# Key loads of the next attention head: all at once, or one with each tile of queries

## The chip, the cores and the metric

The kernel runs on one core of a Trainium2 chip. The metric is the device time of one launch in microseconds (us), the median over several runs. The engines are TensorE (PE, matmuls), VectorE (DVE), ScalarE (ACT), GpSimd (POOL) and SyncE (SP, which here only issues transfers).

## What is computed

One inference step of a one-layer encoder. 16 + 2048 prompt positions and 8 × 16 sample positions of width 1024 are normed and projected by one matrix; eight attention heads of 64 with forget gates, and a short gated convolution beside them, are joined by an output projection. The part that matters here is the attention of the prompt, whose logit has the running sum `c` of the log forget values in it:

```python
p = jnp.einsum('bld,dn->bln', h, w_in)
q, k, v, za, fl, bg, cg, hc, zc = jnp.split(p, SPLIT_IDX, axis=-1)
logf = jax.nn.log_sigmoid((fl + b_f).astype(jnp.float32))
...
s = jnp.einsum('bqhd,bkhd->bhqk', qblk, k) * (DH ** -0.5)
s = s + cq[...] - ck[...]                       # c = cumsum(logf)
s = jnp.where(kpos <= qpos, s, -jnp.inf)
p = jax.nn.softmax(s, axis=-1)
o = jnp.einsum('bhqk,bkhd->bqhd', p, v)
...
cat = jnp.concatenate([o_a * silu(za), y_c * silu(zc)], axis=-1)
xp = xp + jnp.einsum('blm,md->bld', cat, w_out)
```

## The kernel before

All is in float32, each product made of parts in a rounded type (high and low part: `hh`/`hl` of the normed rows, `wh`/`wl` of the weights, `kh`/`kl` of the keys, `qh`/`ql` of the queries). The work runs in two groups of positions. Group 0 is the positions 0 to 1279, group 1 the other 784 with the 128 sample rows. In each group the projection makes queries, keys and values and stores them to DRAM (`qh_d`, `ql_d`, `kh_d`, `kl_d`, `v_d`, the running sums `c_d`) through POOL's queue; attention reads them back.

Attention goes by units of 256 queries: a unit is a head h and a block u, with two tiles of 128 queries. Group 0 has u = 0 to 4 for each of eight heads, 40 units, and unit number n is head (n − 1) // 5, u = (n − 1) % 5; group 1 has u = 5 to 7, units 41 to 64. For each unit a query load of three 64-partition pieces fills `qa` (`qh` twice) and `qb` (`ql`), and two short ones put the sums into `qb`; both tiles are double-buffered by unit. For each head a key load fills `ka` (`kh` and `kl`) and `kb` (`kh`), with two short ones for the sums; these are double-buffered by head. A piece is 64 × 1280 elements in group 0 (320 KB) and 64 × 2064 in group 1 (516 KB). `vb` holds the values of one head. The scores `sp` are two matmuls, `kb` with `qb` and `ka` with `qa`.

Between the attention's steps, PE does the projection of later columns (`ps` from `hh`, `hl`, `wh`, `wl`). Its weights come in blocks `raw` of 512 KB whose loads ACT issues; ACT casts one to `wh`, DVE makes `wl`. All other loads are on SP's queue (q1 in the profile; ACT's is q10, POOL's stores are q0). In turn the loads of SP and ACT take eight semaphores, and each load waits for the one eight before it to have landed.

What sets the order: the kernel is a set of generators, and class `Times` (line 68) keeps a model of each engine's time. `weave` (line 215) lets that generator go on whose next step is ready first by the model, which fixes PE's order; `settle` (line 235) sorts the instructions of each other engine, and SP's transfers, by their time in the model. So a transfer that is asked for at another place changes the model's times and with them the order on every engine. All instructions are recorded through one helper, which is why every row of the profile has line L278.

`scores_of` (line 965) is the generator that asks for keys and queries. When it comes to unit n it asks for the keys of the head itself and of the next one, `load_head` (line 905), and for the queries of this unit and the next, `load_queries` (line 953).

Of the kernel before, what the change touches and what calls it, by code (L numbers as in the profile page):

```python
# [18 lines left out]
DRAM = bass.MemoryType.DRAM  # L19

P = 128
# [5 lines left out]
DH = 64  # L27
# [287 lines left out]
class Step:  # L315
# [4 lines left out]
        for k, v in args.items():  # L320
            setattr(self, k, v)

    def dma(self, out, in_):

        if out.dtype == F32R:
            out = out.bitcast(F32)
        if in_.dtype == F32R:
            in_ = in_.bitcast(F32)
        return getattr(self.nc, STORES if out.space == DRAM else "sync").dma_start(out=out, in_=in_)

    def open(self, ctx, name, side=None, space=None):
        k = {}
# [47 lines left out]
    def load_constants(self, pool):  # L380
        nc, dma = self.nc, self.dma
        mraw = pool.tile([P, P], F32, name="mraw")
        dma(out=mraw, in_=self.cst[:, C_MASK:C_MASK + P])
        nc.vector.tensor_copy(out=self.mask, in_=mraw)
        for i in range(3):
            dma(out=self.cw[:, :, i], in_=self.conv_w[0, i].rearrange("(c p) -> p c", p=P))

        nc.vector.tensor_scalar(out=self.cw, in0=self.cw, scalar1=0.5, scalar2=None, op0=ALU.mult)
# [22 lines left out]
    def normalise(self, ph, xp, bufs, beside=()):  # L411
# [7 lines left out]
        def prepare():  # L419
            i, (pos, rows, ct, col) = todo.pop(0)  # L420
            xt = xp.tile([P, D], F32, name="xt", bufs=bufs)
            if pos == 0:
                dma(out=xt[:NMETA], in_=self.meta_tokens)
                dma(out=xt[NMETA:], in_=self.x_p[:P - NMETA])
            else:
                dma(out=xt[:rows], in_=self.x_s if pos == NPOS else self.x_p[pos - NMETA:pos - NMETA + rows])
            if pos == p0:
                dma(out=g_bc, in_=self.norm_g[0].partition_broadcast(P))
            if beside:
                beside.pop(0)()  # L430
            sq = xp.tile([P, D], BF16, name="sq")
            ss = xp.tile([P, 1], F32, name="ss", bufs=4)
            nc.scalar.activation(out=sq[:rows], in_=xt[:rows], func=AF.Square, accum_out=ss[:rows])
            self.rsqrt(ss[:rows])
            nc.vector.scalar_tensor_tensor(out=xt[:rows], in0=xt[:rows], scalar=ss[:rows, 0:1], in1=g_bc[:rows],
                                           op0=ALU.mult, op1=ALU.mult)
            ahead.append((xt, rows, ct, col, i))
# [465 lines left out]
                self.dma(out=out[a:a + 1, full * P:n], in_=c[t0 + full:t0 + full + 1, :n % P])  # L903

    def load_head(self, ph, h):
        dma = self.dma
        npos = GROUPS[0][1] if ph == 0 else NPOS
        i, p, rows = h % 2, h // 2, slice(DH * (h % 2), DH * (h % 2) + DH)
        ka, kb = self.ka[i], self.kb[i]
        dma(out=ka[0:DH, :npos], in_=self.kh_d[p][rows, :npos])  # L910
        dma(out=ka[DH:P, :npos], in_=self.kl_d[p][rows, :npos])
        dma(out=kb[BR:, :npos], in_=self.kh_d[p][rows, :npos])
        self.sums_rows(kb[2:4], h, 0, self.nk)

    def load_values(self, ph, h):

# [48 lines left out]
    def scores_of(self, ph, st, ready):  # L965

        nc = self.nc
        units = st["units"]
        loaded, asked = 0, 0
        while ph not in self.summed:  # L970
            yield lambda: 0.0 if ph in self.summed else NEVER
        for n, (h, u) in enumerate(units):
            while ("q", h // 2) not in ready:
                yield lambda: 0.0 if ("q", h // 2) in ready else NEVER

            for ahead in range(2):
                if loaded < H and loaded <= h + ahead and ("k", loaded // 2) in ready:
                    self.load_head(ph, loaded)
                    loaded += 1
                if asked < len(units) and asked <= n + ahead and ("q", units[asked][0] // 2) in ready:  # L980
                    self.load_queries(ph, asked, st)
                    asked += 1
            qa, qb, ka, kb = self.qa[n % 2], self.qb[n % 2], self.ka[h % 2], self.kb[h % 2]
            done = []
            for c0, m, nk in self.query_tiles(u):
                while st["tiles"] - st["turned"] >= SB[ph]:
                    yield lambda: 0.0 if st["tiles"] - st["turned"] < SB[ph] else NEVER
                st["tiles"] += 1
                sl = self.ap.tile([P, min(self.nk, NPOS)], F32, name="s", bufs=SB[ph])
                mx = self.ap.tile([P, 8], F32, name="nm", bufs=16)  # L990
                blocks = (nk + P - 1) // P
                nch = (nk + 511) // 512
                ends = [min(nk, (blocks * (x + 1) // nch) * P) for x in range(nch)]
                k0 = 0
                for x, k1 in enumerate(ends):
                    w = k1 - k0
                    yield self.when(qa, qb, ka, kb, slot=(self.sps, "sp"))
                    sp = self.sps.tile([P, 512], F32, name="sp", bufs=SPB)
                    diag = k1 == nk
                    nc.tensor.matmul(sp[:m, :w], qb[:, c0:c0 + m], kb[:, k0:k1], start=True, stop=False)  # L1000
                    nc.tensor.matmul(sp[:m, :w], qa[:, c0:c0 + m], ka[:, k0:k1], start=False, stop=not diag)
                    if diag:
                        nc.tensor.matmul(sp[:m, w - m:w], self.identr[:, :m], self.mask[:, :m], start=False, stop=True)
                    nc.vector.tensor_scalar(out=sl[:m, k0:k1], in0=sp[:m, :w], scalar1=1.0, scalar2=None, op0=ALU.mult,
                                            op1=ALU.max, accum_out=mx[:m, x:x + 1])
                    k0 = k1
                nm = mx[:, 6:8]
                nc.vector.tensor_reduce(out=nm[:m, 0:1], in_=mx[:m, :nch], axis=AX.X, op=ALU.max, negate=True)
                nc.scalar.activation(out=sl[:m, :nk], in_=sl[:m, :nk], func=AF.Exp, bias=nm[:m, 0:1], accum_out=nm[:m, 1:2])
                nc.vector.reciprocal(out=nm[:m, 1:2], in_=nm[:m, 1:2])  # L1010
                done.append((sl, nm))
            st["scored"].append(done)
# [548 lines left out]
STORES = "gpsimd"  # L1561
# [38 lines left out]
BR = 4  # L1600
# [38 lines left out]
```

## Time and profile before

| | us |
|---|---|
| median of 3 runs | 1683.21 (1681.59 to 1683.66) |
| profiled execution, its own time | 1680.57 |
| its span | 1678.7, at a mean granted clock of 0.972 |
| busy: PE / DVE / ACT / POOL | 1564.9 / 861.0 / 632.5 / 481.2 |
| loads on SP's queue, ACT's, stores on POOL's | 106.38, 30.94, 66.96 MB |

The profile is one execution. PE is the engine that is busy nearly all the time; a stretch in which it waits, with what ended the wait, is read from its timeline. The granted clock is TensorE's, as a share of full speed.

### The profile page before, as it was taken

The numbers are of one execution on the slowest core, as the hardware profiler recorded it, in microseconds if no ns is written. First come the engines' busy times: TensorE is split into PE (matmuls) and PEld (weight loads), VectorE is DVE, ScalarE is ACT, GpSimd is POOL, SyncE is SP. The second block draws the span as 40 slices with busy tenths as digits, with TensorE's granted clock in tenths as the row PEclk, the third lists the DMA queues.
The fourth block names the chain that finished last, engine by engine and source line by source line (L and its number), as shares of the span: only waits on it lengthen the run. The fifth ranks groups of instructions, "written<-read, shape, count | busy, mean of one in ns | idle before, by whom it ended". The sixth has DMA issues, their size and how long they took to land.

```text
span 1678.7 us, 27726 instructions
## 1 busy us (share of the span) xinstructions
PE 1564.9 (93%) x10311; PEld 1452.5 (87%) x10311; DVE 861.0 (51%) x2276; ACT 632.5 (38%) x1196; POOL 481.2 (29%) x750
## 2 busy tenths in 40 slices
PE   4789999998999989899995999999999999999996
PEld 4779999998999978899984998998898999868885
DVE  4525667336667557552332666776576673212221
ACT  4314555325553322411111655555554553111221
POOL 2543435523211421225041313212121121223322
PEclk9899999999999998999997999999999999999998
DMA  7446653475432676522237534535534231364442
GB/s 193 118 120 158 155 142 111 113 191 139 105 77 55 219 222 194 153 53 76 40 83 155 137 101 125 127 92 158 140 67 114 37 85 31 88 232 135 142 138 88
DMA packets 159143, 206.06 MB, mean 123 GB/s; under 512 B 22220, under 2 KB 123108, under 8 KB 156320
## 3 DMA queue, kind: packets, MB, share of 16 engines
q1 hardware_dynamic: 73952, 106.38, 22.2%
q10 hardware_dynamic: 61360, 30.94, 11.9%
q0 software_dynamic: 23696, 66.96, 11.5%
q8 instruction: 82, 1.34, 0.3%
q14 instruction: 53, 0.43, 0.1%
HBM read 137.28 MB, written 66.93 MB: 122 GB/s over the span
## 4 chain that ended last, share of the span: by engine, by line
PE 73%; DMA 11%; issue 6%; POOL 3%; DVE 3%; ACT 2%; SPq 1%; ACTq 0%; POOLq 0%; DVEq 0%
PE ps L278 45%; PE sp L278 10%; PE o L278 9%; PE tp L278 8%; DMA raw<-in_w_in_dram 3%; PE tr L278 1%; DMA sqk_d<-el 1%; DMA vb<-v_d 1%; SPq L278 1%; DMA qb<-ql_d 1%; DMA cat_d<-kf 1%; DMA vn<-in_cache_v_dram 1%; DMA gz_d<-kf 1%; DMA o_d<-ol 1%; DMA xt<-in_x_prompt_dram 1%
## 5 line engine op out<-in xcount | busy, mean ns | idle before, releaser
L278 PE MATMUL ps<-hh,wh 128*128 128x256 f32 (+2 forms) x1568 | 502.0, 320 | 20.1 <-DVE el L278 10.0
L278 PE MATMUL ps<-hl,wh 128*128 128x256 f32 (+2 forms) x1568 | 486.3, 310 | 0.0
L278 PE MATMUL ps<-hh,wl 128*128 128x256 f32 (+2 forms) x1568 | 485.9, 310 | 0.0
L278 PEld LDWEIGHTS ps<-hh,wh 128*128 128x128 f32 x1568 | 302.8, 193 | 29.6 <-DVE el L278 10.6
L278 PEld LDWEIGHTS ps<-hl,wh 128*128 128x128 f32 x1568 | 302.6, 193 | 1.6
L278 PEld LDWEIGHTS ps<-hh,wl 128*128 128x128 f32 x1568 | 301.6, 192 | 0.0
L278 DVE TENSOR_TENSOR pl<-tp,ph 128x512 fp32r<-128x512 f32 (+2 forms) x360 | 198.2, 564 | 113.2 <-ACT ph L278 111.3
L278 ACT CAST ph<-tp 128x512 fp32r<-128x512 f32 (+2 forms) x360 | 170.8, 487 | 210.3 <-PE tp L278 197.3
L278 DVE TENSOR_SCALAR_CACHE_REDUCE s<-sp 128x384 f32<-128x384 f32 (+3 forms) x360 | 210.5, 598 | 35.1 <-PE sp L278 33.5
L278 ACT ACTIVATE s<-s,nm 128x128 f32<-128x128 f32 (+16 forms) x136 | 170.5, 1254 | 77.6 <-DVE nm L278 77.0
L278 PE MATMUL tp<-ident,s 128*128 128x128 f32 (+1 forms) x1224 | 191.8, 269 | 0.1
L278 PE MATMUL o<-ph,vb 128*128 128x256 f32 (+4 forms) x584 | 167.6, 306 | 3.4 <-DMA vb<-v_d 3.4
L278 PEld LDWEIGHTS tp<-ident,s 128*128 128x128 f32 (+1 forms) x1224 | 145.0, 140 | 23.9 <-issue 19.9
L278 PE MATMUL sp<-kb,qb 68*128 68x384 f32 (+3 forms) x360 | 143.2, 398 | 18.4 <-DVE s L278 10.8
L278 PE MATMUL o<-pl,vb 128*128 128x256 f32 (+4 forms) x584 | 149.6, 282 | 0.0
L278 PE MATMUL sp<-ka,qa 128*128 128x384 f32 (+3 forms) x360 | 132.7, 369 | 0.0
L278 POOL TENSOR_TENSOR gz<-gz,otmp 64x256 f32<-64x256 f32 (+1 forms) x64 | 47.2, 737 | 273.2 <-DVE otmp L278 253.7
L278 PE MATMUL ps<-o,ch 128*128 128x512 f32 x374 | 118.6, 396 | 2.0 <-DMA o<-o_d 2.0
L278 PEld LDWEIGHTS o<-ph,vb 128*128 128x128 f32 (+1 forms) x584 | 109.9, 188 | 9.1 <-DMA vb<-v_d 2.4
L278 PEld LDWEIGHTS o<-pl,vb 128*128 128x128 f32 (+1 forms) x584 | 110.5, 189 | 0.7
L278 DVE TENSOR_TENSOR wl<-raw,wh 128x1024 fp32r<-128x1024 f32 x56 | 69.0, 1232 | 63.1 <-ACT wh L278 62.4
L278 PE MATMUL ps<-wvh,hh 128*128 128x272 f32 (+3 forms) x288 | 87.2, 303 | 5.0 <-ACT sv L278 4.6
(218 smaller groups left out, 2288.2 us busy)
## 6 DMA issues: line engine op xcount, KB each, us to landing
raw<-in_w_in_dram ACTq DMA_DIRECT2D x59, 512.0 KB
cr<-cat_d SPq DMA_DIRECT2D x17, 512.0 KB
v_d<-vv POOLq DMA_DIRECT2D x32, 256.0 KB, 2.7
vb<-v_d SPq DMA_DIRECT2D x8, 1024.0 KB
oxt<-in_x_prompt_dram SPq DMA_DIRECT2D x16, 512.0 KB
out_dram<-oxt POOLq DMA_DIRECT2D x16, 512.0 KB, 2.9
xt<-in_x_prompt_dram SPq DMA_DIRECT2D x15, 512.0 KB
qa<-qh_d SPq DMA_DIRECT2D x112, 64.0 KB
```

Of the source, the lines that this page charges most:

```text
L278: r = f(*a, **k)
```

## The change

`load_head` no longer makes the transfers of a head's keys: it returns four calls, three for the pieces of `ka` and `kb` and one for the sums. `scores_of` keeps them in a list. Calls of a head that has been reached are made at once; of the next head's, one is made with each tile of queries that is begun. The new argument of `dma` is not used by any call.

```diff
-    def dma(self, out, in_):
+    def dma(self, out, in_, by=None):
...
     def load_head(self, ph, h):
...
-        dma(out=ka[0:DH, :npos], in_=self.kh_d[p][rows, :npos])
-        dma(out=ka[DH:P, :npos], in_=self.kl_d[p][rows, :npos])
-        dma(out=kb[BR:, :npos], in_=self.kh_d[p][rows, :npos])
-        self.sums_rows(kb[2:4], h, 0, self.nk)
+        return [lambda: dma(out=ka[0:DH, :npos], in_=self.kh_d[p][rows, :npos]),
+                lambda: dma(out=ka[DH:P, :npos], in_=self.kl_d[p][rows, :npos]),
+                lambda: dma(out=kb[BR:, :npos], in_=self.kh_d[p][rows, :npos]),
+                lambda: self.sums_rows(kb[2:4], h, 0, self.nk)]
...
-        loaded, asked = 0, 0
+        loaded, asked, parts = 0, 0, []
...
+            while parts and parts[0][0] <= h:
+                parts.pop(0)[1]()
             for ahead in range(2):
                 if loaded < H and loaded <= h + ahead and ("k", loaded // 2) in ready:
-                    self.load_head(ph, loaded)
+                    parts += [(loaded, f) for f in self.load_head(ph, loaded)]
                     loaded += 1
+                while parts and parts[0][0] <= h:
+                    parts.pop(0)[1]()
                 if asked < len(units) and asked <= n + ahead and ("q", units[asked][0] // 2) in ready:
                     self.load_queries(ph, asked, st)
...
                 st["tiles"] += 1
+                if parts:
+                    parts.pop(0)[1]()
```

The order of the instructions moves at these places. On SP's queue in group 0, where the queries of unit 28 (`qa_937`, `qb_939`) and the keys of head 6 (`ka_931`, `kb_933`) are loaded, before:

```order
L278 DMA kb_933<-c_d 1x10x128 x2
L278 DMA qb_939<-c_d 1x2x128
L278 DMA qa_937<-qh_d_94 64x256
L278 DMA ka_931<-kh_d_103 64x1280
L278 DMA ka_931<-kl_d_107 64x1280
L278 DMA kb_933<-kh_d_103 64x1280
L278 DMA qa_937<-qh_d_94 64x256
L278 DMA qb_939<-ql_d_98 64x256
L278 DMA qb_939<-c_d 1x2x128
```

and after:

```order
L278 DMA qa_937<-qh_d_94 64x256
L278 DMA qb_939<-c_d 1x2x128
L278 DMA qa_937<-qh_d_94 64x256
L278 DMA qb_939<-ql_d_98 64x256
L278 DMA qb_939<-c_d 1x2x128
L278 DMA gz<-gz_d_113 64x256
L278 DMA ka_931<-kh_d_103 64x1280
L278 DMA ka_931<-kl_d_107 64x1280
L278 DMA qa_936<-qh_d_95 64x256
```

The three key pieces stood between the two halves of `qa` and ahead of `qb`; now the whole query load goes first, and two of the pieces follow it.

On PE in group 0, the last twelve rows up to the start of unit 13 (its first row is the last shown), before, where 34 rows stand between the end of unit 12 and this start:

```order
L278 MATMUL ps<-hh_130,wl 128x256
L278 MATMUL ps<-hh_132,wh 128x384
L278 MATMUL ps<-hl_133,wh 128x384
L278 MATMUL ps<-hh_132,wl 128x384
L278 MATMUL tp<-ident,s 128x128 x4
L278 MATMUL ps<-hh_132,wh 128x384
L278 MATMUL ps<-hl_133,wh 128x384
L278 MATMUL ps<-hh_132,wl 128x384
L278 MATMUL ps<-hh_132,wh 128x384
L278 MATMUL ps<-hl_133,wh 128x384
L278 MATMUL ps<-hh_132,wl 128x384
L278 MATMUL sp<-kb_933,qb_938 128x256
```

and after, from the row behind unit 12's last one to unit 13's first:

```order
L278 MATMUL ps<-hh_134,wh 128x384
L278 MATMUL ps<-hl_135,wh 128x384
L278 MATMUL ps<-hh_134,wl 128x384
L278 MATMUL o<-ph,vb 128x256
L278 MATMUL o<-pl,vb 128x256
L278 MATMUL o<-ph,vb 128x128
L278 MATMUL o<-pl,vb 128x128
L278 MATMUL tr<-ident,nm 128x128 x2
L278 MATMUL ps<-hh_134,wh 128x384
L278 MATMUL ps<-hl_135,wh 128x384
L278 MATMUL ps<-hh_134,wl 128x384
L278 MATMUL sp<-kb_933,qb_938 128x256
```

Eleven rows now stand between the end of unit 12 and the start of unit 13. Counted from the end of unit 11, which frees the query tile `qb_938`, PE has 83 matmuls before and 63 after; such counts are used below for other units as well (unit 33: 89 and 63, unit 28: 98 and 86, from the end of unit 9 to the start of 11: 100 and 148).

On SP at the start of group 1 (`ka0`, `kb0` are the keys of head 0, `ka1`, `kb1` of head 1; `DMAHW` are the eight semaphores of the loads, `DMASW` those of the stores), before:

```order
L278 DMA kb0_9562<-kh_d0_100 64x2064 [waits DMAHW4_49]
L278 DMA qa0_9565<-qh_d0_92 64x256 [waits DMAHW5_49]
L278 DMA qb0_9567<-ql_d0_96 64x256 [waits DMAHW6_49,DMASW4_49]
L278 DMA ka1_9561<-kh_d0_100 64x2064 [waits DMAHW0_49]
L278 DMA ka1_9561<-kl_d0_104 64x2064 [waits DMAHW1_49]
L278 DMA kb1_9563<-kh_d0_100 64x2064 [waits DMAHW2_49]
L278 DMA qa1_9566<-qh_d0_92 64x256 [waits DMAHW3_49,DMASW6_49]
L278 DMA qa1_9566<-qh_d0_92 64x256 [waits DMAHW4_49]
L278 DMA qb1_9568<-ql_d0_96 64x256 [waits DMAHW5_49,DMASW7_49]
```

and after:

```order
L278 DMA kb0_9562<-kh_d0_100 64x2064 [waits DMAHW4_49]
L278 DMA qa0_9565<-qh_d0_92 64x256 [waits DMAHW5_49]
L278 DMA qb0_9567<-ql_d0_96 64x256 [waits DMAHW6_49,DMASW4_49]
L278 DMA qa1_9566<-qh_d0_92 64x256 [waits DMAHW0_49,DMASW6_49]
L278 DMA qa1_9566<-qh_d0_92 64x256 [waits DMAHW1_49]
L278 DMA qb1_9568<-ql_d0_96 64x256 [waits DMAHW2_49,DMASW7_49]
L278 DMA ka1_9561<-kh_d0_100 64x2064 [waits DMAHW3_49]
L278 DMA ka1_9561<-kl_d0_104 64x2064 [waits DMAHW4_49]
L278 DMA gz_9924<-gz_d0_111 64x256 [waits DMAHW5_49,DMASW0_49]
L278 DMA kb1_9563<-kh_d0_100 64x2064 [waits DMAHW6_49]
L278 DMA vb_9564<-v_d0_108 128x2048 [waits DMAHW7_49]
```

The queries of the second unit moved ahead of head 1's keys, and a re-load `gz` and the values `vb` now stand among and behind these keys.

## Rows read from the trace of the kernel before

**Rows 1.** The page: busy time, share of the span, instructions.
```profile
PE 1564.9 (93%) x10311; PEld 1452.5 (87%) x10311; DVE 861.0 (51%) x2276; ACT 632.5 (38%) x1196; POOL 481.2 (29%) x750
```

**Rows 2.** PE's waits by releaser: total us, times, longest.
```profile
PE sp L278 <- DMA qb<-ql_d: 5.8, 2, 4.3
```

**Rows 3.** PE's timeline, starts of units 8, 13, 28: start, us, [idle before <-releaser].
```profile
191.91 0.36 PE L278 MATMUL sp<-kb,qb 68*128 68x256 f32 x1 [1.54 <-DMA qb<-ql_d]
...
231.21 0.35 PE L278 MATMUL sp<-kb,qb 68*128 68x256 f32 x1 [1.42 <-DMA qb<-c_d]
...
415.31 0.55 PE L278 MATMUL sp<-kb,qb 68*128 68x256 f32 x1 [4.26 <-DMA qb<-ql_d]
```

**Rows 4.** Stretches: us, then PE, PEld, DVE, ACT, POOL, PEclk, DMA share, GB/s.
```profile
415.30:421.00 5.70, 5.69 (x22) 5.70 (x23) 2.56 (x10) 1.41 (x3) 0.00 (x0) 0.52 0.42 134
...
200.00:300.00 100.00, 98.58 (x756) 97.05 (x756) 70.00 (x225) 54.67 (x113) 42.70 (x70) 1.00 0.45 120
...
924.70:929.40 4.70, 4.64 (x21) 4.64 (x21) 3.60 (x10) 2.32 (x6) 1.81 (x3) 0.51 0.59 231
```

**Rows 5.** Issues of SP and ACT (SPq, ACTq) ahead of unit 28.
```profile
399.01 0.50 SPq L278 DMA_DIRECT2D qa<-qh_d  x1
399.62 0.55 SPq L278 DMA_DIRECT2D ka<-kh_d  x1
...
401.47 3.32 SPq L278 DMA_DIRECT2D kb<-kh_d  x1
...
407.64 1.09 SPq L278 DMA_DIRECT2D qb<-ql_d  x1
...
399.86 0.38 ACTq L278 DMA_DIRECT2D raw<-in_w_in_dram  x1
```

**Rows 6.** Query loads of units 3 and 13, and unit 3's first score.
```profile
137.70 1.11 SPq L278 DMA_DIRECT2D qa<-qh_d  x2
...
143.23 0.28 PE L278 MATMUL sp<-kb,qb 68*128 68x256 f32 x1
...
222.06 1.93 SPq L278 DMA_DIRECT2D qa<-qh_d  x2
```

**Rows 7.** Start of group 1: the first key load of head 0, its first score.
```profile
885.62 0.50 SPq L278 DMA_DIRECT2D ka<-kh_d  x1
...
897.65 0.34 PE L278 MATMUL sp<-kb,qb 68*128 68x384 f32 x1
```

**Rows 8.** Timelines at the start of group 1: ACT, PE, DVE, POOL.
```profile
906.60 1.04 ACT L278 CAST wh<-raw 128x1024 fp32r<-128x1024 f32 x1 [14.27 <-DMA raw<-in_w_in_dram]
...
909.43 0.79 PE L278 MATMUL sp<-kb,qb 68*128 68x512 f32 x1 [10.80 <-DVE s L278]
...
911.41 0.08 DVE L278 DVE_READ_ACCUMULATOR s<-sp 128x1 f32 x1
...
913.60 0.44 DVE L278 SCALAR_TENSOR_TENSOR kf<-kf,ps 128x272 f32<-128x272 f32 x1
...
914.33 0.54 POOL L278 DMA_DIRECT2D gz_d<-kf  x1 [20.31 <-DVE kf L278]
...
924.33 0.37 ACT L278 COPY kf<-ps 128x256 f32<-128x256 f32 x1 [6.12 <-DMA gz_d<-kf]
...
924.76 0.69 PE L278 MATMUL tr<-ident,kf 128*128 128x128 f32 x2 [4.47 <-ACT kf L278]
```

**Rows 9.** Queues from 887.9, twice from 896 and 903: packets, MB, share.
```profile
q1 hardware_dynamic: 171, 1.15, 91.3%
...
q1 hardware_dynamic: 187, 1.26, 84.9%
q10 hardware_dynamic: 183, 0.09, 8.9%
...
q10 hardware_dynamic: 595, 0.30, 49.4%
```

**Rows 10.** PE's timeline, group 1, a wait for the values.
```profile
1358.02 0.36 PE L278 MATMUL o<-ph,vb 128*128 128x256 f32 x1 [1.09 <-DMA vb<-v_d]
```

More of the change, by code (lines that the diff above doesn't have):

```diff
@@ L328, in dma @@
             in_ = in_.bitcast(F32)
-        return getattr(self.nc, STORES if out.space == DRAM else "sync").dma_start(out=out, in_=in_)
+        return getattr(self.nc, by or (STORES if out.space == DRAM else "sync")).dma_start(out=out, in_=in_)
     def open(self, ctx, name, side=None, space=None):
```

## The prediction

> **What bounds the kernel now.** I read the page's first part first. TensorE (PE) is busy 93% of the span [rows 1], 1678.7 − 1564.9 = 113.8 us idle, and the change alters neither the number nor the shape of its matmuls. So the time can only move through PE's idle stretches, and through the granted clock of the stretches behind them. Next came the waits of PE by what ended them. Only one line names the loads that this change reorders: 5.8 us in two waits for the query tile qb [rows 2]. PE's timeline places them, 1.54 and 4.26 us, and a third of 1.42 for the sums in qb [rows 3]. They stand before units 8, 28 and 13. Last I read the tables by stretch. With PE full, 756 matmuls take 98.58 us, or 0.130 us each, at clock 1.00; right behind the wait of 4.26 us the clock is 0.52, the lower of its two levels (1.2 GHz), and 22 matmuls take 5.69 us [rows 4].
>
> **The moved loads in group 0.** Before, the three key loads of head 6 stand on SP's queue between the two qa loads of unit 28. Rows 5 show them: qa at 399.01, keys from 399.62 to 401.47 (this one holds SP for 3.32), qb at 407.64; ACT asks for a block of weights at 399.86. PE scores unit 28 at 415.31 [rows 3], 16.3 us after the first issue. The same query chain with no key loads and no weights is issued from 137.70, and unit 3 is scored at 143.23 without a wait, so it takes at most 5.5 us [rows 6]. With weights alone it is issued from 222.06, and the wait at unit 13 ends at 231.21: 9.15 us [rows 3, 6]. Units 8 and 28 are the two where the key loads stood in the chain; the change puts whole query loads ahead of them. What the chain needs must be held against what PE has to do meanwhile. A query tile is free when the unit two before it is scored, so the matmuls between the end of unit n−2 and the start of unit n, counted in the order, times 0.130 us, are its room. Unit 28 has 98 matmuls of room before (12.7 us) and 86 after (11.2 us). 11.2 covers 9.15, so both waits go: −5.80. The slow stretch behind the longer one goes too: 5.69 × (1 − 0.52) = 2.73. **A = −8.5**, bounds 0 (the weights alone hold the chain) and −8.5.
>
> **The moved matmuls in group 0.** The kernel's cost model sees the new transfers and chooses another order of PE from the first unit on. That takes room elsewhere. Unit 13 keeps 63 matmuls of 83 and unit 33 has 63 of 89: 63 × 0.130 = 8.2 us. If the chain again takes 9.15 there, each waits 0.95. The old 1.42 goes, 1.9 come: **B = +0.5**, bounds −1.4 (the weights are not on the queue then) and rival 2 above. No row of before shows what else the new order does; each of its small waits would be like the two of 1.42 and 1.54 [rows 3]. I take two: **E = +3.0**, between 0 and one wait like unit 28's with its clock, 4.26 + 2.73 = 7.0.
>
> The keys themselves come later. Three key loads in group 1 take from 885.62 to a score at 897.65, 12.0 us for 516 KB each [rows 7]; those of group 0 are 320 KB each. Their buffer is free at the end of the unit that last reads it, and head 2's first unit, 11, has 148 matmuls = 19.2 us after the end of unit 9 (100 before). The 12.0 fit, so a later key costs nothing; if this cover is gone, it is rival 3.
>
> **The start of group 1.** Here six key loads, of heads 0 and 1, are issued together. The weights asked for at that time come into wh only at 906.60, PE stands 10.80 us before 909.43 (wl and s follow on DVE), and 4.47 before 924.76, behind a store of kf and its copy [rows 8]. From 887.9 to 893 SP's queue moves 171 packets and the weights' queue no row at all; from 896 to 902 they move 187 and 183 [rows 9]. After, the queries of the second unit stand before head 1's keys, and each of these keys waits for a load eight places before, so part of them comes later than the weights ask. But the head-0 keys, which fill the time until 897, stay. So the weights should land a little sooner: **C1 = −1.5**, of bounds 0 (the value loads that now stand behind take the place) and −6.0 (they begin to move at 890, midway in the first of the two stretches, and not at 896). I take a quarter of that: one of the six key loads now waits until the weights have had their turn.
>
> The second wait has its own chain. The copy of kf on DVE runs at 913.60, though the piece of the score that DVE deals with before it ends at 911.49 [rows 8]; in the new order it stands four instructions earlier, right behind that piece. The store at 914.33 then goes 2.1 us earlier, and so does the copy at 924.33 that waits for it: **C2 = −2.1**. Bounds: −6.7 (4.47 and the 2.27 of the slow stretch behind it, 4.64 × (1 − 0.51) [rows 4]), and +4 (the 1024 KB of values that now go ahead take 12.0 × 1024 / 1548 = 7.9 us at the rate of the keys in [rows 7], half of it where two queues share).
>
> **The last one.** At 1358.02 PE waits 1.09 us for the values vb [rows 10]. They now stand before unit 64's queries: **D = −1.1**, bound 0.
>
> What is left costs nothing: no matmul and no transfer is added, and the calls held back and made one per tile are made when the program is built, not on the chip.
>
> **A rule of the Trainium skill against the trace.** The trace: from 887.9 to 893 the weights' queue moved nothing beside 171 packets of SP's, and from 896 to 902 the two moved 187 and 183; alone, from 903 to 906, the weights reached 595 in 3 us [rows 9]. The Trainium skill, "DMA: Bandwidth & Descriptors", section "Queues, rings and completion order", says that a DMA engine takes turns between the queues that have work, one packet at a time. The later stretch agrees with it, the earlier one does not. By the rule alone the weights should gain most from fewer packets on SP's queue, C1 would be nearer −6 and the time 1669; I keep −1.5 since the earlier stretch contradicts it.
>
> **The sum.** −8.5 + 0.5 + 3.0 − 1.5 − 2.1 − 1.1 = −9.7. The profiled execution took 1680.57 us, 2.64 below the median of 1683.21; 1680.57 − 9.7 = 1670.9, and carried to the median **1673.5**.
>
> **The rivals.**
>
> *1. It was the weights, not the keys.* Unit 13 waited 1.42 with no key load in its chain [rows 3], and a weight load was asked for 0.85 us after unit 28's queries began [rows 5]. If the weights hold the chains, or the keys follow the queries at once and slow the same packets, units 8 and 28 still wait. A = 0 gives −1.2: 1682.0, the same within what can be told. Against it: 16.3 us with keys stand beside 9.15 without.
>
> *2. The room is gone (the slower side).* Units 13 and 33 now have 8.2 us. If their chain takes the 16.3 us of unit 28, because a late key piece meets the weights there, each waits 8.1 and loses 2.73 of clock: 2 × 10.8 = 21.7 in place of the 1.9 in B, so −9.7 + 19.8 = +10.1: **1693.3**. It beats the forecast's gain, and by over 0.2%, from a chain of 13.0 us on: then (13.0 − 8.2 + 2.73) × 2 = 15.1, and −9.7 − 1.9 + 15.1 = +3.5. For it: the queue of weights is asked on ACT's own schedule, near any unit. Against: both chains then have no key load ahead, and the only such chain shown took 9.15.
>
> *3. Keys too late.* A head's last key piece is issued with the fourth tile, one piece per tile. If two heads get it so late that their first unit waits as unit 28 did, that is 2 × (4.26 + 2.73) = 14.0, and −9.7 + 14.0 = +4.3: 1687.5. It decides from 6.6 us a head. Against: 19.2 us of room stand against 12.0 [rows 7]. The Trainium skill's "DMA: Bandwidth & Descriptors", section "Rules for kernel authors", speaks for this rival: issue a transfer early and wait for it late. No row of before shows a late key.
>
> **How the numbers follow.** 0.2% of the time, 3.4 us, is about what a measurement of this kernel can tell from no change. The forecast has 0.57 (faster: even with E at 7.0, or C2 at +4, it stays at −3.6 or less). Rival 1 has 0.23 (same), rival 2 0.15 and rival 3 0.05 (slower). So faster 0.57, same 0.23, slower 0.20. The forecast's own low end is −8.5 − 1.4 + 0 − 6.0 − 2.1 − 1.1 = −19.1: 1664. The range reaches up over rivals 1 and 3 to 1688; it leaves out rival 2 and some 0.05 at the low side.
>
> **What would show it.** Right: no wait at units 8 and 28, a clock near 1.00 behind unit 28, waits of about 1 us or none at units 13 and 33, the wait now at 909.43 between 9 and 10.8 us, the one at 924.76 about 2 us shorter, none at 1358. A is wrong if unit 28 still waits for qb though no key load stands before it. B is wrong if units 13 or 33 wait over 3 us. E is wrong if the new order makes waits elsewhere of over 7 us together. Wrong as a whole: new waits for ka or kb at the first unit of a head.

## The result, and the profile after

The changed kernel takes 1660.39 us (median of 4 runs, 1648.64 to 1663.28) where the kernel before takes 1682.4 (4 runs): ratio 0.9869, 95% interval 0.9832 to 0.9905. That is 22 us faster. The forecast was 9.7 us faster (1673.5, with a range of 1664 to 1688), and the time lies below the range. Single runs of one kernel scatter more than the first three showed: over the 29 runs beside the second set of experiments the kernel before went from 1672.1 to 1690.2, at a median of 1679.4, so only medians of several runs are compared below. Against the later medians of the kernel before, 1679.3 to 1680.4 in five sets of 13 to 29 runs, the same 1660.39 is 19 to 20 us faster. The ratio of an experiment is against the kernel before, run beside it.

The page of after, its span and its busy times (they answer [rows 1]):

```profile
span 1656.3 us, 27721 instructions
PE 1552.8 (94%) x10311; PEld 1442.8 (87%) x10311; DVE 860.5 (52%) x2276; ACT 630.6 (38%) x1196; POOL 483.1 (29%) x750
```

PE is busy 12.1 us less with the same matmuls (the mean granted clock is 0.980 where it was 0.972), and idle 103.5 us where it was 113.8. Four of PE's waits in after by releaser (total, times, longest; they answer [rows 2]):

```profile
PE sp L278 <- DVE s L278: 12.4, 1, 12.4
PE sp L278 <- DMA kn<-in_cache_k_dram: 5.8, 2, 5.1
PE sp L278 <- DMA qb<-c_d: 4.4, 2, 3.9
PE o L278 <- DMA vb<-v_d: 2.5, 2, 2.0
```

No wait for `qb<-ql_d` is left, and no wait at units 8, 13 and 28 [rows 3]. The waits now stand elsewhere. PE's timeline of after:

```profile
161.37 0.66 PE L278 MATMUL sp<-kb,qb 68*128 68x384 f32 x1 [3.86 <-DMA qb<-c_d]
...
375.00 0.53 PE L278 MATMUL o<-ph,vb 128*128 128x256 f32 x1 [2.01 <-DMA vb<-v_d]
...
631.26 0.45 PE L278 MATMUL sp<-ident,kn 128*128 128x128 f32 x1 [5.06 <-DMA kn<-in_cache_k_dram]
...
899.91 0.80 PE L278 MATMUL sp<-kb,qb 68*128 68x512 f32 x1 [12.40 <-DVE s L278]
```

The first stall at the start of group 1 [rows 8] is 12.40 where it was 10.80; the second one, 4.47 before 924.76, is gone. The one at 1358.02 [rows 10] is gone too.

Where the 22 us lie is seen by lost time at equal work. Each matmul gets its usual duration (the 40th percentile, over the traces compared, of the time from the start of one of its form to the next start); the sum of these up to a point of the program is the work done, and the trace's time there minus that sum is what was lost to waits and to the low clock. By stage, against the kernel before, in us:

| stage (work done, us) | before | after | e1 | e2 | e3 | e4 | e5 |
|---|---|---|---|---|---|---|---|
| start (to 100) | 54.0 | +0.1 | +4.4 | −2.0 | +1.8 | −3.9 | −0.6 |
| group 0's attention (to 500) | 39.9 | −1.5 | −6.5 | +12.9 | +1.3 | +0.3 | +1.5 |
| between the groups (to 700) | 29.6 | −8.7 | −2.0 | −9.4 | −8.0 | +0.1 | −6.9 |
| start of group 1 (to 800) | 36.7 | −7.0 | +2.0 | −7.5 | −0.9 | −8.2 | −0.4 |
| the rest | 45.3 | −5.9 | −1.8 | −5.5 | +4.3 | −3.2 | −1.1 |
| sum | 205.5 | −23.0 | −3.9 | −11.5 | −1.5 | −14.9 | −7.5 |

These are single profiled executions. In the first row PE's order is the same in all seven kernels up to 138 us, and it shows that such a figure moves by some 4 us by itself (of e1's +4.4, 1.91 us is a new wait at unit 3). The profiled execution of e3, 1679.23, is the slowest of its nine, whose median is 1670.93; its column shows too little gain. So the forecast looked for the gain in group 0's attention, and it came between the groups, at the start of group 1 and behind it.

### The profile page after: what moved, and what is told of

Its sections match the earlier page's. It is cut to its first block, busy times and chain, and to the rows that moved or that the text cites. A ratio compares the mean times of both kernels' runs of the same rounds, so it can differ in the third digit from the quotient of the medians.

```text
span 1656.3 us, 27721 instructions
## 1 busy us (share of the span) xinstructions
PE 1552.8 (94%) x10311; PEld 1442.8 (87%) x10311; DVE 860.5 (52%) x2276; ACT 630.6 (38%) x1196; POOL 483.1 (29%) x750
## 4 chain that ended last, share of the span: by engine, by line
PE 78%; DMA 10%; issue 4%; POOL 3%; DVE 2%; ACT 2%; SPq 1%; ACTq 0%; POOLq 0%; DVEq 0%
PE ps L278 48%; PE sp L278 11%; PE o L278 10%; PE tp L278 8%; DMA raw<-in_w_in_dram 3%; PE tr L278 2%; DMA sqk_d<-el 1%; DMA vb<-v_d 1%; SPq L278 1%; DMA qb<-c_d 1%; DMA kn<-in_cache_k_dram 1%; DMA ql_d<-el 1%; DVE wl L278 1%; DMA v_d<-vv 1%; DMA qh_d<-eh 1%
## 5 line engine op out<-in xcount | busy, mean ns | idle before, releaser
L278 PEld LDWEIGHTS ps<-hh,wh 128*128 128x128 f32 x1568 | 299.0, 191 | 31.4 <-DVE el L278 11.0
L278 PEld LDWEIGHTS ps<-hl,wh 128*128 128x128 f32 x1568 | 299.1, 191 | 1.7
```

The lines of the kernel that those rows point to most:

```text
L278: r = f(*a, **k)
```

## Experiments: place, order, groups

Two theories were set against each other. Theory P: the place of the keys on SP's queue makes the gain. Theory O: the model's new order of everything else does.

**e1, the place alone.** The kernel before, with the key loads of group 0 sorted 3 us later on SP; PE's order stays.

```diff
-                todo.append((self.times.key, len(todo), r.ins))
+                todo.append((self.times.key + self.times.late, len(todo), r.ins))
...
+        self.nc.late = (3000.0, 0.0)[ph] if h else 0.0
         dma(out=ka[0:DH, :npos], in_=self.kh_d[p][rows, :npos])
```

> The kernel before, its order on PE, DVE, ACT and POOL kept, with one thing changed: in group 0 the three key loads of a head are sorted 3 us later on SP's queue, so that the query loads of units 8 and 28 go ahead of them. Theory P (place on the queue): the waits of 1.54 and 4.26 us at units 8 and 28 and the slow stretch behind unit 28 go, about -8.5 us against the kernel before, 1674; and if the place were the whole effect, -22. Theory O (order of the work): the place alone gives at most 2 us, 1680 to 1683, since the weights load holds the chain as it did at unit 13.

Measured: 1675.39, ratio 0.9968 (0.9952 to 0.9985), −5 us. The waits at units 8 and 28 are gone, though the weights load still stands beside unit 28's queries: it was the keys. But others have come: 1.91 us at unit 3, 1.02 for `vb` at 200.75, and these two (PE's timeline of e1):

```profile
366.71 0.36 PE L278 MATMUL sp<-kb,qb 68*128 68x256 f32 x1 [1.91 <-DMA qb<-c_d]
...
423.95 0.39 PE L278 MATMUL o<-ph,vb 128*128 128x256 f32 x1 [2.85 <-DMA vb<-v_d]
```

The four are 7.7 us together, as much as the three of [rows 3] that went (7.2); the gain that can be placed is in the clock, which is 1.00 from 400 to 450 us in e1 and 0.93 before. SP asks for the last of these `vb` at 417.56, behind a key piece and 1.4 us later than before, and PE, which no longer stands at unit 28, comes to it sooner. P is right on the waits that go and too high in the size: −5, not −8.5.

**e2, the order alone.** The changed kernel, the pieces of group 0 sorted 6 us earlier.

```diff
+        def early(out, in_):
+            self.nc.late = -6000.0 if ph == 0 and h else 0.0
+            dma(out=out, in_=in_)
+            self.nc.late = 0.0
```

> The changed kernel, its order on PE kept, with the key loads of group 0 sorted 6 us earlier on SP's queue, so that they stand again inside or ahead of query loads (of several units, not just of 8 and 28). Theory P: the query loads are late again, waits for qb of 1.5 to 4 us at two units or more, and 8 us of the gain are given back: about 1669. Theory O: it stays within 3 us of the changed kernel, about 1660.

Measured: 1671.18, ratio 0.9953 (0.9938 to 0.9968): 11 us of the gain are given back, in group 0's attention (+12.9 in the table), by waits like these (PE's timeline of e2):

```profile
227.21 0.66 PE L278 MATMUL sp<-kb,qb 68*128 68x384 f32 x1 [3.53 <-DMA qb<-ql_d]
...
434.74 0.66 PE L278 MATMUL sp<-kb,qb 68*128 68x384 f32 x1 [4.96 <-DMA qa<-qh_d]
```

All other stages keep their gain. So a key load in a query chain costs about what the prediction said (three waits that the changed kernel has not, of 1.78, 3.53 and 4.96 us, where [rows 3] has 1.54 and 4.26); and what the changed kernel gained outside this stage has nothing to do with the place of group 0's keys.

**e3 and e4, one group each.**

```diff
-                    parts += [(loaded, f) for f in self.load_head(ph, loaded)]
+                    parts += [(loaded if ph == 0 else 0, f) for f in self.load_head(ph, loaded)]
```

(e4: `ph == 1`.) Expected of e3 and of e4:

> The change in group 0 alone; in group 1 all key loads of a head are made at once as before. The changed kernel gained 22 us, by the lost time at equal work 1 to 2 of them in group 0's attention, 12 between the groups, 7 at the start of group 1 and 5 late in it. If the group-0 part makes the middle stretch, as both theories say, this kernel keeps 10 to 14 us of the gain, about 1668 to 1672; if the stall at the start of group 1 comes from group 1's own loads (as predicted), it stands here as before, 10.8 and 4.5 us.

> The change in group 1 alone; group 0 as before, instruction for instruction. If the stall at the start of group 1 comes from the six key loads issued together, it gets shorter here by the 7 us seen in the changed kernel, and 5 us more come late in group 1: about 1670. If those gains came from how the work stands when group 1 begins, which group 0 decides, nothing is gained: 1680 to 1683.

Measured: e3 1670.93, ratio 0.9953 (0.9934 to 0.9972); e4 1667.01, ratio 0.9925 (0.9907 to 0.9943). −0.47% and −0.75% add up to −1.22%, nearly the whole 1.31%. The second stall at the start of group 1 answers to group 1's keys alone. In e3 it stands (first line; 2.70 for 4.47 before), in e4 only the first stall is left (second line):

```profile
919.33 0.33 PE L278 MATMUL tr<-ident,kf 128*128 128x128 f32 x1 [2.70 <-ACT kf L278]
...
904.18 0.79 PE L278 MATMUL sp<-kb,qb 68*128 68x512 f32 x1 [9.63 <-DVE s L278]
```

**e7 and e9, keys together but behind the queries.** e7 is the kernel before with two calls exchanged; e9 does that in group 0 and spreads in group 1.

```diff
+                if asked < len(units) and asked <= n + ahead and ("q", units[asked][0] // 2) in ready:
+                    self.load_queries(ph, asked, st)
+                    asked += 1
                 if loaded < H and loaded <= h + ahead and ("k", loaded // 2) in ready:
                     self.load_head(ph, loaded)
                     loaded += 1
```

```diff
                     self.load_queries(ph, asked, st)
                     asked += 1
+            while parts and ph == 0:
+                parts.pop(0)[1]()
```

> The kernel before with two calls exchanged: the queries of the unit are asked for first, and then all key loads of the next head together. Nothing is spread over the tiles. If what counts is that queries go ahead of keys, this gains what the change gains, 1660 within 5 us, though in another order of PE; if the spreading counts, the three key loads together hold up the values or the next queries, and it stays at 1675 to 1682.

> In group 0 the queries of the unit are asked for first and then all pieces of the next head's keys at once; in group 1 one piece with each tile, as in the change. From the lost time at equal work of the earlier runs: group 0 with keys together behind the queries lost some 8 us less than before by its end, and the change in group 1 alone gained 11 to 13. If the effects of the two groups add up: -19 to -21 against before, about 1659 to 1661, though the middle stretch (the wait for x) stays as before. If the 12 us that the change gained between the groups come only with the pieces spread in group 0, this ends there, at 1660 or more.

Measured: e7 1680.62, ratio 1.0012 (0.9989 to 1.0036); e9 1695.38, ratio 1.0092 (1.0059 to 1.0126), a miss by 35 us. PE's timeline of e7 (first line) and of e9 (the others):

```profile
1239.72 0.55 PE L278 MATMUL o<-ph,vb 128*128 128x256 f32 x1 [7.92 <-DMA vb<-v_d]
...
165.60 0.58 PE L278 MATMUL o<-ph,vb 128*128 128x256 f32 x1 [10.36 <-DMA vb<-v_d]
...
645.75 0.45 PE L278 MATMUL sp<-ident,kn 128*128 128x128 f32 x1 [10.17 <-DMA kn<-in_cache_k_dram]
```

The two waits for `vb` are not made by the keys. The last key load ahead of these values was asked for at 1194.99 in e7 and at 125.61 in e9, 28 and 23 us before them; a weights load was asked for 1.8 and 1.0 us before them (ACT's and SP's issues, e7 first, then e9):

```profile
1221.42 0.37 ACTq L278 DMA_DIRECT2D raw<-in_w_in_dram  x1
...
1223.18 0.32 SPq L278 DMA_DIRECT2D vb<-v_d  x1
...
147.61 0.38 ACTq L278 DMA_DIRECT2D raw<-in_w_in_dram  x1
...
148.64 0.39 SPq L278 DMA_DIRECT2D vb<-v_d  x1
```

From 1222.5 to 1232 in e7 the weights' queue moved 880 packets and no other queue one. So these two kernels do not show that the three pieces have to be spread. And e9 asks for group 0's keys in the same manner as e7 and lost 22.6 us in group 0's attention, where e7 gained 6.6 by the same reckoning: the orders that follow from it differ by more than the effect under study.

## Experiments: is it the change or the order?

The model's start cost of a transfer (500) was set to another value in both kernels. No call moves, but 1874 to 5831 of PE's 10311 rows then hold another matmul (by tile and shape). This measures what an order is worth.

```diff
-DMA_START = 500.0
+DMA_START = 450.0
```

> The kernel before, its model's start cost of a transfer set to 450 in place of 500; no call is moved, but the model orders the work anew (11275 lines of PE's listing differ). Theory O (luck of the order): orders of the same work lie some 10 us apart, so this lands anywhere from 1665 to 1690. Theory P: without a change of place it stays within 4 us of before, 1676 to 1684.

> The changed kernel with the same 450 in the model (10934 lines of PE's listing differ from the changed kernel's). Theory O: it lands anywhere from 1650 to 1680, and the distance to the run before this one is not the 22 us of the change. Theory P: the place of the keys makes the gain in any order, so it is 15 to 25 us faster than the run before this one.

> The kernel before with the model's start cost of a transfer at 550. Together with the next run a third pair of orders. Theory P (the change gains in any order): before in three orders lies at 1680 to 1690. Theory O (luck): it may be as fast as the change, 1665 or less.

> The changed kernel with 550. Theory P: 15 to 27 us faster than the run before this one, as in the two pairs so far (22 and 27). Theory O: the distance is anything from -10 to 30.

> The kernel before with the model's start cost at 475, the first of a fourth pair. Three pairs stand so far: -22 (500), -27 (450), +14 (550). Theory O: anywhere from 1665 to 1695. Theory P, weakened by the pair at 550: 1678 to 1690.

> The changed kernel at 475. If the change gains mostly and 550 was the odd one, it is 15 to 27 us faster than the run before this one, 1655 to 1668. If the sign is a matter of the order, anything from 1655 to 1690.

Measured, us; the lost time at equal work by stage is after minus before:

| start cost | before | after | change | group 0's attention | between | start of group 1 | rest |
|---|---|---|---|---|---|---|---|
| 450 | 1690.53 | 1663.5 | −27 | −7.9 | −9.3 | −7.9 | +2.5 |
| 475 | 1688.79 | 1677.5 | −11 | −5.1 | +2.1 | −8.8 | +0.8 |
| 500 | 1682.4 | 1660.39 | −22 | −1.5 | −8.7 | −7.0 | −5.9 |
| 550 | 1666.7 | 1680.79 | +14 | +15.7 | +3.5 | −2.2 | −1.8 |

The same change is worth −27 to +14 us; the mean of the four is −11.5 (single stages of a pair are good to some 4 us, as above). The kernel before alone moves by 24 us with a constant that says nothing of the hardware. Theory P, in the form that the change gains in any order, falls with the pair at 550, and the kernel before at 450 lies outside its 1676 to 1684. Three lines of e13 and e14 (550, before and after) show what an order does. PE waits for the cached keys `kn` of the sample rows in both, 8.53 and 11.05 us; the values in group 0 are late only in the second (last line):

```profile
628.79 0.45 PE L278 MATMUL sp<-ident,kn 128*128 128x128 f32 x1 [8.53 <-DMA kn<-in_cache_k_dram]
...
648.45 0.45 PE L278 MATMUL sp<-ident,kn 128*128 128x128 f32 x1 [11.05 <-DMA kn<-in_cache_k_dram]
...
247.37 0.58 PE L278 MATMUL o<-ph,vb 128*128 128x256 f32 x1 [5.45 <-DMA vb<-v_d]
```

One stage has the same sign in every pair: the start of group 1 (at 550, −2.2, it is within the scatter). Against the kernel before it is 6 to 9 us shorter in each kernel that spreads group 1's keys, in whatever order (after, e2, e4, e6, e9, e10, e12, e14, e16, e18: −7.0, −7.5, −8.2, −7.1, −6.1, −6.7, −7.7, −6.7, −9.2, −6.9), and within 3 us of it where they are issued together (e1, e3, e5, e7, e8, e11, e15, e17); only e13 is 4.5 us shorter without the change. The gain between the groups has no such pattern.

**e15, the group-0 part in another order** (the edit of e3, with a start cost of 450).

> The change in group 0 alone, with 450 in the model, beside the kernel before at 450 (1690.5) and the changed one at 450 (1663.5). If the spreading in group 0 makes the gain between the groups in any order, this keeps about half of the 27 us, 1674 to 1680, and no wait for x as the group-0 part had at 500. If it was luck there, it lies at 1684 to 1692, with the wait for x of some 4.3 us.

Measured: 1670.7, ratio 0.9947 (0.9919 to 0.9975), against 1690.53 for the kernel before at 450. It keeps the gain between the groups (8 to 11 us less than e11 there, by the traces that the usual durations are taken from), with no wait for x. So at 450 and 500 that gain does come with the group-0 part; at 475 and 550 the changed kernel has none of it against its pair. In each of these orders PE waits for some load there: 4.24 us for x in before, 5.06 for `kn` in after, 10.41 and 10.36 for `kn` at 475 (before and after), 8.53 and 11.05 at 550, and at 450 two waits for `kn` of 8.37 and 7.57 before, one of 5.36 for `vo`, the values of the sample rows, after. Each of these loads was asked for 0.7 to 6.7 us behind a weights load. Why an order sets the one behind the other stays open; what such a neighbour costs is tried next.

## Experiments: a weights load in front of a short one

What are the waits between the groups made of? In the kernel before, the first tile of x for group 1 is asked for 1.43 us after a weights load (ACT's and SP's issues, ACT's first use, PE's wait):

```profile
677.93 0.37 ACTq L278 DMA_DIRECT2D raw<-in_w_in_dram  x1
...
679.36 0.34 SPq L278 DMA_DIRECT2D xt<-in_x_prompt_dram  x1
...
688.29 1.06 ACT L278 ACTIVATE sq<-xt 128x1024 bf16<-128x1024 f32 x1 [5.03 <-DMA xt<-in_x_prompt_dram]
...
691.70 0.69 PE L278 MATMUL sp<-ident,xt 128*128 128x128 f32 x2 [4.24 <-DVE xt L278]
```

In after the weights load stands behind it, and the tile is used 3.98 us after its issue, not 8.93:

```profile
666.04 0.34 SPq L278 DMA_DIRECT2D xt<-in_x_prompt_dram  x1
...
670.02 1.05 ACT L278 ACTIVATE sq<-xt 128x1024 bf16<-128x1024 f32 x1
...
671.41 0.38 ACTq L278 DMA_DIRECT2D raw<-in_w_in_dram  x1
```

Theory W says that this is the cause. Each of the next kernels moves one weights load on ACT's queue, by its number k, and nothing else.

```diff
+        if queue == "scalar":
+            self.nc.late = 8000.0 if self.nc.fetched == 22 else 0.0
+            self.nc.fetched += 1
         getattr(self.nc, queue).dma_start(out=raw, in_=self.w_v[:, :, n0:n0 + P])
+        self.nc.late = 0.0
```

**e5** (k = 22, in the kernel before):

> The kernel before with one instruction moved: the weights load that ACT issues at 677.93, 1.4 us before the first x tile of group 1 is asked for at 679.36, now stands on ACT behind the first square of that tile. Every other engine's order is as before. Theory W (a weights load holds up what is asked for shortly after it): the tile lands about 4 us after its issue and not 9, PE's wait of 4.24 us at 691.70 and the slow stretch of 6.8 us behind it go, -5 to -7.6 us at that place, about 1674 by the median of before in the same call. Theory O (PE had too little other work there): the wait stays within 1 us of 4.24.

Measured: 1673.22, ratio 0.9965 (0.9949 to 0.9981), −6 us, at the place that was named. The rows of e5:

```profile
678.89 0.34 SPq L278 DMA_DIRECT2D xt<-in_x_prompt_dram  x1
...
682.74 1.05 ACT L278 ACTIVATE sq<-xt 128x1024 bf16<-128x1024 f32 x1
...
682.78 0.37 ACTq L278 DMA_DIRECT2D raw<-in_w_in_dram  x1
...
686.93 1.04 PE L278 MATMUL sp<-ident,xt 128*128 128x128 f32 x8
```

The tile is in use 3.85 us after its issue and PE does not wait for it. W is shown here: one transfer, issued 4.8 us later, gives 6 us. The clock has its share, by the seventh column of the windows behind this point, of before and of after; 0.60 is a stretch in which the lower level (1.2 GHz) held most of the time, behind the wait of 4.24:

```profile
691.70:698.50 6.80, 6.80 (x28) 6.80 (x29) 5.22 (x7) 3.09 (x7) 2.69 (x4) 0.60 0.29 106
...
673.90:680.00 6.10, 6.10 (x42) 6.03 (x41) 4.30 (x7) 4.10 (x10) 2.38 (x4) 1.00 0.82 255
```

**e6** (k = 4, 4 us later, in the changed kernel, at the wait of 3.86), **e16** (k = 20, 16 us later, in the changed kernel, at the wait of 5.06), **e8** (k = 34, 6 us later, in the kernel before, at the second stall of group 1) and **e10** (e9 with k = 22):

> The changed kernel with one instruction moved: the weights load that ACT issues at 147.60, in the middle of the query load of unit 5, goes behind it, to about 152.6. Theory W: the wait of 3.86 us for qb at 161.37 and most of the slow stretch of 6.8 us behind it go, -4 to -7 us against the changed kernel, about 1654 to 1656. If the wait there is made by the key and value loads on SP's own queue, it stays at 3 to 4 us and the time at 1660.

> The changed kernel with one instruction moved: the weights load that ACT issues at 614.38, ahead of the cache loads asked for at 621.04 and 621.98, goes behind them, to about 630. Its weights are first used at 649.15. Theory W: the wait of 5.06 us for the cached keys at 631.26 and the slow stretch of 3.4 us behind it go, -5 to -6.8, about 1654, faster than both kernels. Otherwise the wait stays and the time is 1660.

> The kernel before with one instruction moved: the weights load that ACT issues at 908.94 goes behind the copy at 913.19, that is, to about the time of the store of kf at 914.33. Theory W: the store lands some 5 us after its issue and not 10, ACT's copy at 924.33 comes earlier, and the second stall of 4.47 us at the start of group 1 shrinks to 0 to 1, -4 to -6.7 us at that place, if the weights themselves do not come too late. If the store is held up by the value and query loads on SP's queue, the stall stays.

> The kernel of the run before this one with the weights load ahead of group 1's x tiles moved behind the second square on ACT. Theory W: the wait of about 4.4 us for x and the slow stretch behind it go, -5 to -7, about 1653 to 1655, which would be faster than the change. Theory O: no difference to the run before this one.

Measured: e6 1660.95 and e16 1660.39 (the changed kernel: 1660.39), e8 1682.98, ratio 1.0021 (0.9999 to 1.0043), e10 1696.39 (e9: 1695.38). None gained. In e6 and e16 the wait at the named place went and came back at the next loads behind the weights. In e6 (first line) that is the query load of unit 6. In e16 it is `vo` and a block `oraw` of the output weights, both asked for 7 us behind the moved load; ACT's copy to `om` stands behind its cast of `oraw` (the other two lines):

```profile
169.35 0.30 PE L278 MATMUL sp<-kb,qb 68*128 68x128 f32 x1 [3.09 <-DMA qb<-c_d]
...
645.48 0.46 PE L278 MATMUL o<-vo,pth 16*128 16x512 f32 x1 [2.74 <-DMA vo<-vs_d]
...
651.71 0.48 PE L278 MATMUL tr<-ident,om 128*128 128x128 f32 x1 [4.03 <-ACT om L278]
```

e10's order had no wait for x to begin with. In e8 the weights were meant to go behind the store of kf and did not: ACT reached them before POOL reached the store.

```profile
914.80 0.37 ACTq L278 DMA_DIRECT2D raw<-in_w_in_dram  x1
...
917.26 0.54 POOL L278 DMA_DIRECT2D gz_d<-kf  x1 [20.93 <-DVE kf L278]
...
929.08 0.37 ACT L278 COPY kf<-ps 128x256 f32<-128x256 f32 x1 [6.88 <-DMA gz_d<-kf]
...
929.51 0.47 PE L278 MATMUL tr<-ident,kf 128*128 128x128 f32 x1 [5.24 <-ACT kf L278]
```

The copy that needs the store runs 14.3 us after the weights' issue here, and 15.4 us after it in the kernel before (908.94 in its trace to 924.33 [rows 8]), wherever the store stands between. That fits W, but no run has the weights load behind the store.

## Why the prediction was wrong, point by point

**The step that failed is E.** It gave the moved order a one-sided term, +3.0 between 0 and +7.0: new small waits would come, and no old ones would go but those of A to D. The runs show a two-sided term several times as wide. The order takes group 0's attention from −7.9 to +15.7 us and the stretch between the groups from −9.3 to +3.5 over four pairs. In the pair that was measured first, it was −8.7 between the groups and −5.9 in the rest.

By stage, the forecast was −5.0 in group 0's attention (A, B and E), and −1.5 was measured; −3.6 at the start of group 1 (C1 and C2), and −7.0; −1.1 behind it (D), and −5.9; nothing between the groups, and −8.7. The −8.7 is the gain of e5's kind: there one weights load, no longer in front of x, gave 6 us at that place, and the prediction had no term for such a neighbour. Most of the −5.9 stays open. E fails by its own sign as well: the new waits of 3.86, 2.01 and 5.06 us are 10.9 together. The moved order of all this, from the first unit to the end, was priced by two rows. A range that took the order in would have been some ±20 us, and then the forecast's −9.7 stands beside a mean of −11.5 over four orders. That is no proof that its terms were right; C2 was not. The low end, 1664, also took C2 at −2.1 and not at its own bound of −6.7; with it the sum is −23.7 and the end 1659.5, below the measured time. That would have been the right number with the gain between the groups still missing.

**A, −8.5.** The cause was right: with the keys behind the queries in the old order (e1) both waits go. Its size was not: −6.5 at that stage and −5 in the median, since PE then stands at the next loads that are not there yet, 7.7 us in four waits. In after the two waits went as well, and unit 5 (3.86 us and 2.75 of clock) and `vb` at 375.00 (2.01) took nearly all of it back. The prediction followed its own chain and no load behind it. Rival 1 (it was the weights) falls with e1 at units 8 and 28.

**B, +0.5.** Unit 13 does not wait; no wait came at 13 or 33, so rival 2 did not happen at these units. A chain nearly as long as its 16.3 us came at unit 5, 15.3 us from the first issue at 146.03 to the score at 161.37, with a wait of 3.86 and a granted clock of 0.68 behind it (the window of after). No key piece stands in that chain; in e6, with the weights load moved out of it, unit 5 does not wait.

```profile
161.40:170.00 8.60, 8.60 (x42) 8.60 (x43) 4.75 (x16) 3.08 (x6) 2.59 (x4) 0.68 0.28 84
```

Rival 3 (late keys) did not happen: no new wait for ka or kb stands in after.

**C1, −1.5.** The first stall did not shrink in a way that can be told: 12.40 in after, 9.63 in e4, 10.80 before. Head 1's keys behind the queries did not bring the weights sooner: from their issue to the cast into wh they take 20.0 us in after (877.12 to 897.08) and 18.7 before (887.93 to 906.60). Two readings behind the term were wrong. The weights' packets begin at 893, not 896 (first line, the kernel before from 893 to 896), and the 595 packets from 903 to 906 [rows 9] did not move alone (second line, SP's queue in that stretch):

```profile
q10 hardware_dynamic: 205, 0.10, 13.2%
...
q1 hardware_dynamic: 222, 0.20, 33.4%
```

**C2, −2.1: mis-sized, by its reason.** The whole second stall went, 4.47 and the slow stretch, the bound of −6.7. The store did go earlier, 2.71 us behind the end of the first stall where it was 4.90, as predicted; but what counts is another row. In the order of ACT with its waits (`DMASW4` is that store), the third copy waits for the store before, and the fourth after:

```
COPY kf_10049<-ps_10010 128x256 [waits DMASW4_49,PE_49]
COPY kf_10137<-ps_10095 128x272 [waits PE_49,Activation_49]

COPY kf_10039<-ps_9986 128x256 [waits PE_49,Activation_49]
COPY kf_10133<-ps_10051 128x272 [waits DMASW4_49,PE_49]
```

`kf` has two buffers, and the moved rows changed which copy takes the one that is being stored. The prediction could have read that from the order alone. The same two pictures stand in the orders of all the kernels: the third copy waits for the store in each of the ten that issue group 1's keys together, in none of the ten that spread them. PE's wait for that copy is 4.47 us before, 3.35 in e1, 2.70 in e3, 3.34 in e5, 5.24 in e8, 2.93 in e11, 3.76 in e15 and 4.19 in e17; it is in none of the ten others, and not in e7 and e13, where the third copy does wait for the store but PE has no wait for it. This part of the gain, 6 to 9 us at the start of group 1, is the one that belongs to the change in nearly every order, though it too comes by the order that the model makes and not by a key that lands sooner.

**D, −1.1.** Right in after; but at 450 and 475 the changed kernel waits 3.37 and 1.69 us at the same place, and the kernel before at 450 and 550 does not wait there, so it hangs on the order.

## What to carry to other kernels

Where a planner orders the whole program from a cost model, a change of one request is a change of order, and its effect is the wanted one plus a draw that here spread over some 40 us; before crediting an idea, perturb a constant of the model in both kernels and compare the pairs. What holds in all pairs, and has a row in the order that explains it, can be credited to the idea. Look for the needed transfers that stand just behind a large load on another queue, and expect that the wait may only move to its neighbour: of the three moves that took a weights load out of the way, one gained and two did that.

## What the runs showed of the hardware

A weights load (512 KB in packets of 512 bytes) can hold up what other queues ask for after it; e5 shows the price, 8.93 us to the use of a tile where it takes 3.85 without. From the profile's list of queues (packets, MB, share), the stretches from 910 to 919 in before, from 618 to 626 in after and from 916 to 925 in e8:

```profile
q10 hardware_dynamic: 795, 0.41, 54.7%
...
q10 hardware_dynamic: 673, 0.34, 49.7%
...
q10 hardware_dynamic: 804, 0.41, 56.3%
```

No other queue moved a packet in them, though SP had asked for queries at 914.64 (before) and for cached keys at 621.04 (after), POOL for a store at 914.33 (before) and at 917.26 (e8), and the 16 engines were half idle. The weights move 84 to 89 packets per us there, and 198 in [rows 9] from 903 to 906, with SP's queue beside them. It is not so in every stretch: from 399 to 408 in before the weights' queue moved 851 packets, SP's 221 and POOL's 161. The Trainium skill, "DMA: Bandwidth & Descriptors", section "Queues, rings and completion order", has each engine take turns between the queues that it has work for; in the three stretches the trace shows no turn. Whether the work of the other queues had reached the engines by then, and which part of the path the load keeps to itself, is not shown here. The other way round, with keys asked for ahead of them, the weights waited [rows 9].
